# Second-part matmuls on 64 rows are widened to 128 rows in a float32r decoder layer

## The chip, the core and the metric

The kernel runs on one core of a Trainium2 chip. The metric is the device time of one execution in microseconds (us). The profile is of one execution on that core; a row of it names the engine (PE is TensorE's matmuls, PEld its weight loads, DVE is VectorE, ACT is ScalarE, POOL is GpSimd), the line of the kernel, the operation and the tiles out<-in.

## The reference, cut to what matters

One layer: RMSNorm, one wide input projection split into five branches, each branch with its own mixer, a gated merge, an output projection and a final RMSNorm. The tokens are 512, the model is 1024 wide, each branch 512. The change touches two of the branches.

```python
def stick_breaking_attention(q, k, v):          # 8 heads of 64 channels
    ...
        z = jnp.einsum('bhqd,bhkd->bhqk', qf[:, :, q0:tk], kf[:, :, :tk]) * scale
        ...
        later = lax.cumsum(log_keep, axis=3, reverse=True) - log_keep
        w = jnp.where(strict, jnp.exp(jax.nn.log_sigmoid(z) + later), 0.0)
        outs.append(jnp.einsum('bhqk,bhkd->bhqd', w, vf[:, :, :tk]))

def rg_lru(x, w_a, b_a, w_x, b_x, lam):         # 8 blocks of 64 channels
    xb = xf.reshape(b, s, NB_D, BW_D)
    r = jax.nn.sigmoid(jnp.einsum('bsnc,ncd->bsnd', xb, w_a.astype(jnp.float32)).reshape(b, s, e) + b_a)
    i = jax.nn.sigmoid(jnp.einsum('bsnc,ncd->bsnd', xb, w_x.astype(jnp.float32)).reshape(b, s, e) + b_x)
```

## The kernel before, in words

Every matmul operand is kept as two float32r parts, a first part (hi) and a second part (lo), whose sum is the float32 value. A product of two such values takes three matmuls in `mm3` (L178: hi by hi, L179: hi by lo, L180: lo by hi). Weights arrive by DMA as float32 (`wst`), ACT makes the first part (`whi`, L158) and DVE the second (`wlo`, L159); there are four buffers of each.

A string of steps (`STEPS`) lists the program's pieces in the order in which they are written: `bp0` to `bp3` project the queries, keys and gates of a pair of attention heads (`b_pair_proj`), `ba0` to `ba7` are the eight heads (`b_head`), `dt0` to `dt3` the four tiles of the RG-LRU gates (`d_tile`), `G` and `U` gate and up-projection steps of the merge, `cv`, `cp`, `ch` the mLSTM. A scheduler then interleaves the instructions of neighbouring steps on each engine by priority, so that the small matmuls of a head stand between the big ones of the merge. Each engine runs its list in order.

In `b_head` a head has 64 channels, which fill half of the 128 rows. The queries' tile `qq` holds the first part in the head's own half of the rows and the second part in the other half; the keys' tile `kk2` holds the first part in both halves. One matmul on 128 rows (L561) so gives the product of both parts of the queries with the first part of the keys. The product of the queries' first part and the keys' second part is a matmul on the head's own 64 rows (L562); the second parts of both heads of a pair share one tile, `kl`. A head has four such pairs of matmuls, of 512, 384, 128 and 256 columns, into `zb` banks. ACT makes sigmoids of the logits (L566 to L570), POOL masks them (L574), DVE runs the scan (L581) and the product (L582), PE transposes the weights of the attention (L591, into `wb`), ACT and DVE split them (L593, L594) into three hi and lo pairs of tiles, and PE multiplies them with the values (L605, into the single `po` bank).

The RG-LRU does the same with its blocks of 64 channels: `xx` holds both parts of a block's input in the two halves of the rows, `wh` the weights' first part in both halves, and L880 is a matmul on 128 rows, L881 the second part of the weights on 64. `d_setup` loads the weights into both halves of the rows and splits all 128 rows, so the second part already stands in both.

The tiles `q`, `k`, `kl` and the split attention weights come from one pool, `opool`, of 14 tiles of 128x512. Each evacuation in `b_pair_proj` works on 64 rows: L533 and L534 for the queries, L539, L540 (ACT) and L541 (DVE) for the keys.

Of the kernel before, what the change touches and what calls it, by code (L numbers as in the profile page):

```python
# [26 lines left out]
# section starts in w_in's columns  # L27
# [7 lines left out]
# channel-major column tiles of w_in, one [128, 8, 128] unit each  # L35
# [4 lines left out]
# columns of the packed per-channel constants  # L40
# [10 lines left out]
# blocks of the [key, query] triangle: key block j holds queries from 128 j on  # L51
TRI = {0: (0, 0, 512), 1: (1, 0, 384), 3: (1, 384, 128), 2: (2, 0, 256)}   # j: bank, offset, width
BANKW = (512, 512, 256)
PAIRS = [(i, j) for j in range(NT) for i in range(j, NT)]                  # (query block, key block)
# [27 lines left out]
def build(ctx, tc, x, memT, cols_d, rows_d, wcm, wbv, wcv0, wcv1, wmk, wmv, wup, wout, dw, fg, out):  # L82
# [14 lines left out]
    # ---------------------------------------------------------------- constants  # L97
# [14 lines left out]
    with tc.tile_pool(name="setup", bufs=1) as sp:  # L112
        t2 = sp.tile([P, P], F32, name="t_b")
        V.memset(t2, 1.0 / 512)
        V.tensor_copy(ones512, t2)
        t4 = sp.tile([P, P], F32, name="t_d")
        V.memset(t4, 0.0)
        # 0 where s <= t, -1e30 elsewhere   (partition s, free t)
        G.affine_select(out=cmask, in_=t4, pattern=[[1, P]], compare_op=ALU.is_ge, fill=-1e30, base=0,
                        channel_multiplier=-1)  # L120
# [9 lines left out]
    # ---------------------------------------------------------------- pieces  # L130
    def rsqrt(v, pool):
        """1 / sqrt(v) of a few columns, the table's root refined by a Newton step"""
        n = v.shape[1]
        s = pool.tile([P, n], F32, tag=f"rsq_s{n}", name="rsq_s", bufs=2)
        t = pool.tile([P, n], F32, tag=f"rsq_t{n}", name="rsq_t", bufs=2)
        act(s, v, AF.Sqrt, scale=0.25)
        V.reciprocal(t, s)
        V.tensor_tensor(out=t, in0=t, in1=v, op=ALU.mult)
        V.scalar_tensor_tensor(out=s, in0=t, scalar=0.25, in1=s, op0=ALU.mult, op1=ALU.add)
        V.reciprocal(t, s)  # L140
        return t
# [4 lines left out]
    def load_w(src, n, scale=None, stage=wpool):  # L146
        """a weight unit [128, n] in two halves of split operands: [(hi, lo), (hi, lo)]"""
# [19 lines left out]
    def piece(w, k, n, per, o=0, c=None):  # L167
        """columns of block k (n wide, per blocks in a half) of both parts"""
# [5 lines left out]
    def mm3(ps, terms, first=True, last=True, check=False):  # L174
        """terms: list of (lhsT hi, lhsT lo, rhs hi, rhs lo); three float32r passes each"""
# [6 lines left out]
    def proj(c, scale=None):  # L182
        """one 128-channel tile of the input projection, [channel, token], without its bias"""
# [10 lines left out]
    def split_sb(f, hi, lo):  # L194
        """f: float32 view of lo's own storage or another tile"""
# [13 lines left out]
    def vtile():  # L209
        """room for two split operands of 1024 columns (or mLSTM's values with their ones)"""  # L210
# [6 lines left out]
    # the array's clock rises after some microseconds of work: start it while the first loads run  # L217
# [4 lines left out]
    # ---------------------------------------------------------------- norms of mem and x  # L222
# [46 lines left out]
    # mem's projections take its rows' 1 / rms afterwards  # L269
# [73 lines left out]
    def op_pair():  # L343
        return op(), op()
# [19 lines left out]
    # ---------------------------------------------------------------- A: gated conv module  # L364
# [19 lines left out]
    def log_exp_tables(after):  # L384
        """one table set with both, loaded after the ACT instruction given"""
# [3 lines left out]
    def chan_mean(tiles, name):  # L389
        """mean over the channels of four tiles, on every partition"""  # L390
# [37 lines left out]
    # ---------------------------------------------------------------- M: memory attention  # L428
# [46 lines left out]
    # ---------------------------------------------------------------- token-major values  # L475
    def v_half(src, n):
        """[128 tokens, n] per token tile for n weight columns, without their bias"""
# [19 lines left out]
    # ---------------------------------------------------------------- B: stick-breaking attention  # L497
# [13 lines left out]
    def b_v(half):  # L511
        # per token tile and pair of heads: first parts of the even head, both second parts, first parts of the odd head
# [13 lines left out]
    def b_pair_proj(p):  # L526
        """per head 128 rows: the queries' two parts, and the keys' first part twice; and the keys' second parts"""
        q, k, kl = op_pair(), op_pair(), op()
# [8 lines left out]
        with tc.high_priority(offset=EVAC):  # L537
            for h, r in enumerate(HALF):
                act(k[h][r], ps[r], AF.Identity, bias=b[r])  # L539
                act(k[h][HALF[1 - h]], ps[r], AF.Identity, bias=b[r])  # L540
                V.scalar_tensor_tensor(out=kl[r], in0=ps[r], scalar=b[r], in1=f32(k[h][r]),  # L541
                                       op0=ALU.add, op1=ALU.subtract)
# [3 lines left out]
    def b_head(pp, hh):  # L546
        p, q, k, kl, z = pp
        qq, kk2 = q[hh], k[hh]
# [4 lines left out]
        for b, ts in enumerate(((3,), (2, 0), (1,))):  # L553
            # logits [query, key] of query blocks ts, keys up to the block's own
            z_ps = at.tile([P, S], F32, tag="at", name="zb")
            o = 0
            for t in ts:
# [4 lines left out]
                mm(d, lhsT=qq[r, tsl], rhs=kl[r, :n], start=False, stop=True, skip_group_check=True)  # L562
# [8 lines left out]
            for t in ts:                    # keys before the query alone  # L571
# [4 lines left out]
        for t in (3, 2, 0, 1):  # L576
# [3 lines left out]
            # products of what later keys leave, from the last key to the first (factors in [0, 1]: the min keeps them)  # L580
# [21 lines left out]
        for j in range(NT):                 # the head's rows take the values' first parts, the others the second  # L602
# [9 lines left out]
    # ---------------------------------------------------------------- C: mLSTM  # L612
# [4 lines left out]
    def c_v(half):  # L617
        # per token tile and head: values, ones (with a zero), the values' second part
# [23 lines left out]
    def c_gates():  # L642
        """running maxima, in-block sums of log f, and the exponents' two parts"""
# [14 lines left out]
        for t in range(NT):                # log f <= 0: the min keeps the sum  # L658
# [10 lines left out]
        # sums of whole blocks between key block j and query block i  # L669
# [157 lines left out]
    # ---------------------------------------------------------------- D: RG-LRU  # L827
    def d_rates(after):
        """8 log sigmoid(lambda), per channel"""
# [5 lines left out]
        # log1p(e) = 2 atanh(e / (2 + e)), e = exp(-|lam|) <= 1  # L835
# [16 lines left out]
    def d_setup():  # L852
        # per block of 64 channels both gates' weights side by side, first parts in both halves of the rows
# [9 lines left out]
    def d_tile(i):  # L863
# [9 lines left out]
        for b, h in enumerate(HALF):  # L873
            o = HALF[1 - b]
            xx = op()                       # both parts of a block's input
# [5 lines left out]
            mm(ps, lhsT=wl[h, sl], rhs=xx[h], start=False, stop=True)  # L881
# [8 lines left out]
    def d_scan(tiles):  # L890
        for i, r, ig, th, z in tiles:
            act(r, r, AF.Exp, scale=dst_["sc"][:, i:i + 1])
        # 1 - exp(2 l) = -tanh(l) (1 + exp(2 l))
# [16 lines left out]
    # ---------------------------------------------------------------- merge  # L910
# [29 lines left out]
    # ---------------------------------------------------------------- program  # L940
# [56 lines left out]
    # ---------------------------------------------------------------- output projection  # L997
# [31 lines left out]
    for half in range(2):  # L1029
        if half:  # L1030
            wo = [hl for k2 in range(4) for hl in load_out(1, k2)]
        for t in range(NT):
            tsl = slice(t * P, (t + 1) * P)
            parts = 2 if half and t == NT - 1 else 1          # the last tile in two
            w = S // parts
            for c in range(parts):
# [9 lines left out]
                # mean of squares so far, with eps  # L1046
# [17 lines left out]
def _layout(a):  # L1064
# [3 lines left out]
    def chan(v):                       # [n * 128] -> [128, n]  # L1068
        return v.reshape(-1, P).T
# [7 lines left out]
    def tok(s, n):                     # [2 halves of k, 128, 4, n]  # L1077
# [16 lines left out]
    def bd(w):                         # [8, 64, 64] -> [2, 64, 4, 64]: block 2 t + b at [b, :, t]  # L1094
# [26 lines left out]
```

## Time and profile before

| what | value |
|---|---|
| median of 3 runs | 866.03 us (865.93 to 866.09) |
| span of the profiled execution, first to last instruction | 864.6 us |
| PE busy | 853.6 us, 99% of the span |
| weight loads busy | 703.9 us, 81% |
| DVE busy | 624.3 us, 72% |
| ACT busy | 449.1 us, 52% |
| POOL busy | 38.7 us, 4% |
| mean granted TensorE clock | 0.997 |

The profiled execution's own time is its span, 864.6 us, and the little that lies around it; the median of the timed runs is 1.4 us above the span. Busy matmuls overlap in the profile, since a matmul's duration includes its way through the array, so the distance from one matmul's start to the next one's start says more than the duration.

### The profile page before, as it was taken

How to read it: one execution, taken by the hardware profiler on the slowest of the kernel's cores; microseconds unless marked ns; L12 is line 12 of the kernel's file. 1: busy time of each engine (PE TensorE's matmuls, PEld its weight loads, DVE VectorE, ACT ScalarE, POOL GpSimd, SP SyncE). 2: the span in 40 equal slices, each digit the busy share in tenths (PEclk: the TensorE clock that was granted, in tenths of full speed). 3: DMA queues.
4: the chain of work that ended last, by engine and by line, in shares of the span. 5: the costliest groups of instructions: out<-in, count | busy, mean ns of one | idle time of the engine just before them, and what ended most of it. 6: DMA issues, size and time to landing. Idle time of an engine off the chain costs nothing.

```text
span 864.6 us, 11346 instructions
## 1 busy us (share of the span) xinstructions
PE 853.6 (99%) x4100; PEld 703.9 (81%) x4100; DVE 624.3 (72%) x1198; ACT 449.1 (52%) x814; POOL 38.7 (4%) x83
## 2 busy tenths in 40 slices
PE   8999999999999999999999999999999999999996
PEld 7888888888898889777778888888888787788886
DVE  7979999999466587776676768668767665555744
ACT  5734456434364453566344445456355766763523
POOL 3000000000000111010231000000000000000000
PEclk9999999999999999999999999999999999999999
DMA  8332222222223121222122233332232222233612
GB/s 324 123 99 96 83 88 74 73 98 98 98 76 101 69 89 60 98 74 87 60 73 63 87 120 110 99 121 74 74 110 74 97 77 94 74 105 115 209 60 98
DMA packets 24145, 84.31 MB, mean 98 GB/s; under 512 B 2709, under 2 KB 2837, under 8 KB 24089
## 3 DMA queue, kind: packets, MB, share of 16 engines
q1 hardware_dynamic: 24088, 83.59, 28.4%
q8 instruction: 32, 0.52, 0.3%
q14 instruction: 25, 0.20, 0.1%
HBM read 81.47 MB, written 2.11 MB: 97 GB/s over the span
## 4 chain that ended last, share of the span: by engine, by line
PE 98%; DMA 1%; DVE 1%; ACT 0%; SPq 0%; issue 0%; ACTq 0%
PE pj L178 27%; PE pj L179 27%; PE pj L180 27%; PE pj L494 2%; PE pj L492 2%; PE pj L493 2%; PE zb L562 1%; PE po L605 1%; PE wb L591 1%; PE zb L561 1%; DMA mt<-in 1%; PE og L795 1%; PE pj L317 0%; PE pj L318 0%; PE tp L466 0%; PE dps L881 0%
## 5 line engine op out<-in xcount | busy, mean ns | idle before, releaser
L158 ACT ACTIVATE whi<-wst 128x512 fp32r<-128x512 f32 (+1 forms) x256 | 160.6, 631 | 287.5 <-PE pj L179 231.9
L179 PE MATMUL pj<-hL,whi 128*128 128x512 f32 x768 | 303.1, 395 | 0.0
L180 PE MATMUL pj<-hH,wlo 128*128 128x512 f32 x768 | 302.9, 395 | 0.0
L178 PE MATMUL pj<-hH,whi 128*128 128x512 f32 x768 | 302.8, 394 | 0.0
L159 DVE TENSOR_TENSOR wlo<-wst,whi 128x512 fp32r<-128x512 f32 (+1 forms) x256 | 176.6, 692 | 108.8 <-ACT whi L158 99.4
L180 PEld LDWEIGHTS pj<-hH,wlo 128*128 128x128 f32 x768 | 144.4, 188 | 33.5 <-issue 1.0
L179 PEld LDWEIGHTS pj<-hL,whi 128*128 128x128 f32 x768 | 144.4, 188 | 32.7 <-issue 0.5
L178 PEld LDWEIGHTS pj<-hH,whi 128*128 128x128 f32 x768 | 144.4, 188 | 32.4 <-issue 0.2
L380 DVE SCALAR_TENSOR_TENSOR acc<-u,cols,acc 128x512 f32<-128x512 f32 x120 | 88.1, 747 | 0.8
L178 PE MATMUL pj<-yH,whi 128*128 128x512 f32 x160 | 63.5, 398 | 0.0
L179 PE MATMUL pj<-yL,whi 128*128 128x512 f32 x160 | 63.0, 394 | 0.0
L180 PE MATMUL pj<-yH,wlo 128*128 128x512 f32 x160 | 62.9, 394 | 0.0
L178 PEld LDWEIGHTS pj<-yH,whi 128*128 128x128 f32 x160 | 30.0, 188 | 7.5 <-issue 0.5
L180 PEld LDWEIGHTS pj<-yH,wlo 128*128 128x128 f32 x160 | 30.1, 188 | 6.8
L179 PEld LDWEIGHTS pj<-yL,whi 128*128 128x128 f32 x160 | 30.1, 188 | 6.6
L574 POOL TENSOR_SCALAR_AFFINE_SELECT kp<-kp 128x128 f32<-128x128 f32 x32 | 14.3, 461 | 401.5 <-ACT kp L566 401.2
L581 DVE TENSOR_TENSOR_SCAN kp<-kp 128x512 f32<-128x512 f32 (+3 forms) x32 | 26.6, 854 | 7.5 <-POOL kp L574 7.3
L494 PE MATMUL pj<-whi,hL 128*128 128x256 f32 (+1 forms) x112 | 31.5, 283 | 0.0
L493 PE MATMUL pj<-wlo,hH 128*128 128x256 f32 (+1 forms) x112 | 31.5, 282 | 0.0
L492 PE MATMUL pj<-whi,hH 128*128 128x256 f32 (+1 forms) x112 | 31.3, 283 | 0.0
L922 ACT ACTIVATE g<-pj,cols 128x512 f32<-128x512 f32 x40 | 27.2, 679 | 2.1 <-DVE merged L938 1.5
L936 DVE TENSOR_TENSOR g<-g,pj 128x512 f32<-128x512 f32 x32 | 21.8, 682 | 8.6 <-PE pj L180 8.5
(306 smaller groups left out, 1188.0 us busy)
## 6 DMA issues: line engine op xcount, KB each, us to landing
wst<-in SPq DMA_DIRECT2D x138, 512.0 KB, 3.3
xt<-in SPq DMA_DIRECT2D x4, 512.0 KB, 10.6
merged<-in SPq DMA_DIRECT2D x4, 512.0 KB, 4.4
out<-merged SPq DMA_DIRECT2D x8, 256.0 KB, 2.3
wst<-in SPq DMA_DIRECT2D x2, 528.0 KB, 4.1
mt<-in SPq DMA_DIRECT2D x2, 512.0 KB, 5.8
f<-crow SPq DMA_DIRECT2D x4, 256.0 KB, 3.6
rows<-in SPq DMA_DIRECT2D x1, 518.0 KB, 10.3
```

Of the source, the lines that this page charges most:

```text
L158: act(hi[:, :m], f, AF.Copy)
L159: V.tensor_tensor(out=lo[:, :m], in0=f, in1=f32(hi[:, :m]), op=ALU.subtract)
L178: mm(ps, lhsT=ah, rhs=bh, start=first and i == 0, stop=False, skip_group_check=check)
L179: mm(ps, lhsT=ah, rhs=bl, start=False, stop=False, skip_group_check=check)
L180: mm(ps, lhsT=al, rhs=bh, start=False, stop=last and i == n - 1, skip_group_check=check)
L380: V.scalar_tensor_tensor(out=a, in0=u[:, k:k + S], scalar=col("a_w", i * 31 + k), in1=a, op0=ALU.mult, op1=ALU.add)
L492: mm(dst[t], lhsT=hH[:, k, tsl], rhs=wh, start=first, stop=False, skip_group_check=True)
L493: mm(dst[t], lhsT=hH[:, k, tsl], rhs=wl, start=False, stop=False, skip_group_check=True)
L494: mm(dst[t], lhsT=hL[:, k, tsl], rhs=wh, start=False, stop=k == NK - 1, skip_group_check=True)
L581: V.tensor_tensor_scan(kk, kk, kk, 1.0, op0=ALU.mult, op1=ALU.min)
L922: act(g, ps, AF.Sigmoid, bias=b)
L936: V.tensor_tensor(out=merged[:, d, :] if first else g, in0=g, in1=ps, op=ALU.mult)
```

## The change

The queries' tile and the RG-LRU's input tile are unchanged. The keys' second part gets a tile of its own for each head, in which it stands in both halves of the rows (two DVE instructions of 64 rows per head in place of one). L562 then takes all 128 rows of the queries (first and second part) and of the keys' second part, and L881 all 128 rows of the weights' second part and of the input. Each adds one product that was left out before, second part by second part. The rest of the diff takes comments out, which are not shown here.

```diff
     def b_pair_proj(p):
-        """per head 128 rows: the queries' two parts, and the keys' first part twice; and the keys' second parts"""
-        q, k, kl = op_pair(), op_pair(), op()
+
+        q, k, kl = op_pair(), op_pair(), op_pair()
...
             for h, r in enumerate(HALF):
                 act(k[h][r], ps[r], AF.Identity, bias=b[r])
                 act(k[h][HALF[1 - h]], ps[r], AF.Identity, bias=b[r])
-                V.scalar_tensor_tensor(out=kl[r], in0=ps[r], scalar=b[r], in1=f32(k[h][r]),
-                                       op0=ALU.add, op1=ALU.subtract)
+                for o in HALF:
+                    V.scalar_tensor_tensor(out=kl[h][o], in0=ps[r], scalar=b[r], in1=f32(k[h][r]),
+                                           op0=ALU.add, op1=ALU.subtract)
...
-        qq, kk2 = q[hh], k[hh]
+        qq, kk2, kl2 = q[hh], k[hh], kl[hh]
...
                 mm(d, lhsT=qq[:, tsl], rhs=kk2[:, :n], start=o == 0, stop=False, skip_group_check=True)
-                mm(d, lhsT=qq[r, tsl], rhs=kl[r, :n], start=False, stop=True, skip_group_check=True)
+                mm(d, lhsT=qq[:, tsl], rhs=kl2[:, :n], start=False, stop=True, skip_group_check=True)
...
             mm(ps, lhsT=wh[:, sl], rhs=xx, start=True, stop=False)
-            mm(ps, lhsT=wl[h, sl], rhs=xx[h], start=False, stop=True)
+            mm(ps, lhsT=wl[:, sl], rhs=xx, start=False, stop=True)
```

The changed kernel has one line more from L541 on, so the old L541 is L542 there, L561 and L562 are L562 and L563, L594 is L595, L605 is L606, and L881 is L882. The order of POOL's and SP's instructions is the same; on PE, ACT and DVE it differs around the attention branch. Three places follow.

On DVE, at the evacuation of the keys of the second pair of heads (`bp1`), the list before is:

```order
L534 SCALAR_TENSOR_TENSOR op<-pj,bq_99,op 64x512 x2
L159 TENSOR_TENSOR wlo<-wst,whi 128x512 x2
L541 SCALAR_TENSOR_TENSOR op<-pj,cols,op 64x512
L159 TENSOR_TENSOR wlo<-wst,whi 128x512
L541 SCALAR_TENSOR_TENSOR op<-pj,cols,op 64x512
L159 TENSOR_TENSOR wlo<-wst,whi 128x512
```

and with the change:

```order
L534 SCALAR_TENSOR_TENSOR op<-pj,bq_99,op 64x512 x2
L159 TENSOR_TENSOR wlo<-wst,whi 128x512 x2
L542 SCALAR_TENSOR_TENSOR op<-pj,cols,op 64x512 x2
L159 TENSOR_TENSOR wlo<-wst,whi 128x512
L542 SCALAR_TENSOR_TENSOR op<-pj,cols,op 64x512 x2
L159 TENSOR_TENSOR wlo<-wst,whi 128x512
```

Nothing moves there; each second part of the keys is made twice, in one go, between the same weight units.

On DVE again, in the first head that runs (`ba2`), these are the weight unit that PE's next big matmuls need (`wlo`, 528 columns), the last product of the scan, and the splits of the attention weights, with what each waits for. Before:

```order
L159 TENSOR_TENSOR wlo_2888<-wst_2885,whi_2887 128x528 [waits DMAHW4_49,Activation_49]
L582 TENSOR_TENSOR f_2745<-f_2745,kp02_589 128x256 [waits DVE_49,Pool_49]
L594 TENSOR_TENSOR op_2765<-wb_2759,op_2764 128x512 [waits Activation_49]
L594 TENSOR_TENSOR op_2774<-wb_2768,op_2773 128x512 [waits Activation_49]
L594 TENSOR_TENSOR op_2781<-wb_2777,op_2780 128x256 [waits Activation_49]
L159 TENSOR_TENSOR wlo_2892<-wst_2885,whi_2891 128x528 [waits Activation_49]
```

With the change:

```order
L159 TENSOR_TENSOR wlo_2894<-wst_2891,whi_2893 128x528 [waits DMAHW4_49,Activation_49]
L583 TENSOR_TENSOR f_2751<-f_2751,kp02_589 128x256 [waits DVE_49,Pool_49]
L595 TENSOR_TENSOR op_2771<-wb_2765,op_2770 128x512 [waits Activation_49]
L595 TENSOR_TENSOR op_2780<-wb_2774,op_2779 128x512 [waits Activation_49]
L595 TENSOR_TENSOR op_2787<-wb_2783,op_2786 128x256 [waits DVE_49,PE_49,Activation_49]
L159 TENSOR_TENSOR wlo_2898<-wst_2891,whi_2897 128x528 [waits Activation_49]
```

The third split now also waits for PE. Two pairs of heads hold two tiles more of the 14 than before, and the last tile of this head comes free only when the first value matmuls have read theirs.

On PE, a little later, this is the end of `ba2`'s value matmuls and the start of the next head's logits (`ba1`). Before:

```order
L605 MATMUL po<-op,v 128x384
L605 MATMUL po<-op,v 128x256
L494 MATMUL at<-whi,hL 128x264
L605 MATMUL po<-op,v 128x256
L605 MATMUL po<-op,v 128x128 x2
L492 MATMUL at<-whi,hH 128x264
L493 MATMUL at<-wlo,hH 128x264
```

With the change, the rows at the end of the same stretch are:

```order
L494 MATMUL at<-whi,hL 128x264
L562 MATMUL zb<-op 128x512
L606 MATMUL po<-op,v 128x256
L606 MATMUL po<-op,v 128x128 x2
L563 MATMUL zb<-op 128x512
L562 MATMUL zb<-op 128x384
```

The matmul of 256 columns that reads the late tile, and the two of 128 columns after it, move six big matmuls and one logit matmul down. In `ba6` they move down by eight big matmuls in the same way.

## Rows read from the trace of the kernel before

**Rows 1.** The page: span, busy time by engine, the chain that ended last.
```profile
span 864.6 us, 11346 instructions
...
PE 853.6 (99%) x4100; PEld 703.9 (81%) x4100; DVE 624.3 (72%) x1198; ACT 449.1 (52%) x814; POOL 38.7 (4%) x83
...
PE 98%; DMA 1%; DVE 1%; ACT 0%; SPq 0%; issue 0%; ACTq 0%
```

**Rows 2.** Timeline of PE, first head's logits: start us, duration us, line, tiles.
```profile
289.11 0.40 PE L561 MATMUL zb<-op 128*128 128x512 f32 x1
289.44 0.50 PE L562 MATMUL zb<-op 64*128 64x512 f32 x1
289.86 0.44 PE L561 MATMUL zb<-op 128*128 128x384 f32 x1
...
291.42 0.38 PE L562 MATMUL zb<-op 64*128 64x256 f32 x1
291.74 0.50 PE L178 MATMUL pj<-yH,whi 128*128 128x512 f32 x1
292.07 0.39 PE L179 MATMUL pj<-yL,whi 128*128 128x512 f32 x1
```

**Rows 3.** Timeline of the weight loads (PEld) at the same place.
```profile
288.88 0.19 PEld L561 LDWEIGHTS zb<-op 128*128 128x128 f32 x1
289.43 0.18 PEld L562 LDWEIGHTS zb<-op 64*128 64x128 f32 x1 [0.36 <-issue]
289.86 0.19 PEld L561 LDWEIGHTS zb<-op 128*128 128x128 f32 x1 [0.25 <-issue]
```

**Rows 4.** Timeline of PE, an mLSTM head's twelve score matmuls, three per width.
```profile
527.61 0.39 PE L769 MATMUL zb<-op 128*128 128x512 f32 x1
527.84 0.40 PE L770 MATMUL zb<-op 128*128 128x512 f32 x1
...
529.52 0.39 PE L178 MATMUL pj<-yH,whi 128*128 128x512 f32 x1
```

**Rows 5.** Timeline of PE, one RG-LRU block.
```profile
745.54 0.40 PE L880 MATMUL dps<-op,v 128*128 128x512 f32 x1
745.87 0.49 PE L881 MATMUL dps<-op,v 64*128 64x512 f32 x1
746.29 0.50 PE L180 MATMUL pj<-hH,wlo 128*128 128x512 f32 x1
746.63 0.39 PE L880 MATMUL dps<-op,v 128*128 128x512 f32 x1
```

**Rows 6.** Instructions of L562 and L881: count, ns least/median/most, first and last start, forms.
```profile
L562 PE MATMUL zb<-op x32: 323/409/498, 289.4 to 468.7; 64*128 64x512 f32 x8, 64*128 64x384 f32 x8, 64*128 64x128 f32 x8, 64*128 64x256 f32 x8
L881 PE MATMUL dps<-op,v x8: 491/492/502, 669.6 to 746.9; 64*128 64x512 f32 x8
```

**Rows 7.** Instructions of L541 and L534, the 64-row splits on DVE.
```profile
L541 DVE SCALAR_TENSOR_TENSOR op<-pj,cols,op x8: 741/750/758, 198.6 to 401.2; 64x512 fp32r<-64x512 f32 x8
L534 DVE SCALAR_TENSOR_TENSOR op<-pj,bq,op x8: 744/750/755, 192.9 to 392.2; 64x512 fp32r<-64x512 f32 x8
```

**Rows 8.** Timeline of DVE while the second pair's keys are evacuated.
```profile
280.11 0.74 DVE L541 SCALAR_TENSOR_TENSOR op<-pj,cols,op 64x512 fp32r<-64x512 f32 x1 [0.71 <-ACT op L540]
281.45 0.69 DVE L159 TENSOR_TENSOR wlo<-wst,whi 128x512 fp32r<-128x512 f32 x1 [0.60 <-ACT whi L158]
282.86 0.76 DVE L541 SCALAR_TENSOR_TENSOR op<-pj,cols,op 64x512 fp32r<-64x512 f32 x1 [0.71 <-ACT op L540]
```

**Rows 9.** Timeline of ACT, DVE and PE between the first head's logits and transposes.
```profile
289.69 0.67 ACT L922 ACTIVATE g<-pj,cols 128x512 f32<-128x512 f32 x1
290.26 0.59 ACT L566 ACTIVATE kp<-zb 128x512 f32<-128x512 f32 x1
...
296.69 0.70 DVE L159 TENSOR_TENSOR wlo<-wst,whi 128x528 fp32r<-128x528 f32 x1
...
297.84 0.37 PE L493 MATMUL pj<-wlo,hH 128*128 128x264 f32 x1
```

**Rows 10.** The same two ends in a later head: DVE's product, PE's transpose.
```profile
334.32 0.73 DVE L582 TENSOR_TENSOR f<-f,kp 128x384 f32<-128x384 f32 x2
...
337.16 0.27 PE L591 MATMUL wb<-ident,f 128*128 128x128 f32 x1
```

## The prediction

> **What bounds the kernel now.** I read the page first: PE is busy for 99% of the span, and the chain that ended last is PE for 98% of it [rows 1]. So a microsecond taken from PE's list counts as a microsecond of the end, as long as the others keep up. Busy time alone doesn't tell what PE loses, because matmuls overlap; so I went on to the timeline of PE around the lines that change and looked at the distance between starts. At full pace a 512-column matmul starts 0.23 us after the one before it: the mLSTM's L769 and L770 start at 527.61 and 527.84 [rows 4]. In the attention head the steps are longer. L562 (64 rows) starts 0.33 after L561, the next L561 (128 rows) 0.42 after that, and the first big matmul behind the group, L178, is followed only after 0.33 [rows 2]. The weight loads say why: the first L561, which follows another matmul on 128 rows, has its load begun at 288.88, 0.23 before it starts itself, so under the matmul before it; the load of L562 begins at 289.43, just as L562 starts, after 0.36 us in which the load side waited for nothing that the profile shows, and the load of the following L561 again waits 0.25 [rows 3]. So PE does not overlap across a change between 64 and 128 rows, in either direction. L562 runs 32 times and L881 8 times, all on 64 rows and all among matmuls on 128 [rows 6].
>
> **The change part by part.**
>
> *The switches.* First head: from the first L561 at 289.11 to L178 at 291.74 the eight logit matmuls take 2.63 us, and L178's own step is 0.10 longer than 0.23, together 2.73 [rows 2]. What the same eight take on 128 rows stands in the mLSTM: twelve matmuls of the same four widths, three of each, from 527.61 to 529.52, which is 1.91 [rows 4]. Two of three is 1.27. Saved: 2.73 - 1.27 = 1.46 us a head, 8 heads, 11.7. In some heads other small matmuls stand between the pairs; a pair then still has two switches, so I keep the figure. RG-LRU: L880, L881 and the matmul behind them take 0.33, 0.42 and 0.34, that is 1.09 [rows 5], against three steps of 0.23, 0.69 [rows 4]; saved 0.40 a block, 8 blocks, 3.2. Sum 14.9.
>
> The bounds. Above: if the narrow matmuls ran at the pace of the wide ones by columns (0.23 us for 512), the eight would take 1.15 and a head would save 1.58; with the RG-LRU 15.8. Below: if none of the 128- and 256-column matmuls could start closer than one weight load lasts, 0.19 [rows 3], and 384 neither, the eight would take 2 x (0.23 + 3 x 0.19) = 1.60 and a head would save 1.13, in all 12.2. I take 14.9, since the mLSTM rows are the same shapes on the same engine.
>
> A rule speaks against this gain. The row: a 64-row L881 costs its block 0.40 more than three equal steps [rows 5]. The Trainium skill, TensorE: Matmul & The Clock Gate, in its table on why this matters for your kernels, says that a single matmul over few rows takes the time of one over 128, and that the way to gain is to place several in distinct row groups so that they run at once. By that rule the width costs nothing either way and the sum would be 0; it is a rival below. The trace agrees with it for the matmul itself, not for its place between wider ones.
>
> *The second splits on DVE.* L541 was 8 x 0.75 us; now it is 16, the added eight into the other half of the rows. The trace has that form too: L534 reads one half and writes the other, also 0.75 [rows 7]. That is 6.0 us more of DVE in the whole run, against 0 on the path: in the second pair DVE sat idle for 0.71, 0.60 and 0.71 between these very instructions [rows 8], and each gap takes most of one. In the first pair DVE is full of convolution taps, which are behind by 3.0 us then; the order gives PE other steps there. If all of it came on the path it would cost 6.0; I take 0. ACT's work is unchanged, and `d_setup` did not change at all.
>
> *The extra tile.* A pair of heads now holds six of the 14 `opool` tiles. In `ba2` and `ba6` the third split of the attention weights waits for the head's own first value matmuls, and the order has moved its reader six or more matmuls down. That is over 1 us at 264 or 512 columns, and the split is one instruction on DVE. Queued behind it on DVE is the next weight half. I take 0, and price the other end as a rival.
>
> *Where PE now arrives early.* Between a head's logits and its transposes lies a way through ACT, POOL and DVE that gets no shorter. In `ba2` ACT is busy without a gap from 289.69 into the first sigmoid at 290.26, so this can't start earlier; DVE, in order behind the scans, makes the next `wlo` from 296.69 to 297.39, and PE uses it at 297.84, a lead of 0.45 [rows 9]. With PE 1.46 earlier, it waits 1.0. In `ba0`, the tightest of the other heads by what I read, DVE's product is done at 335.05 and its transpose starts at 337.16, a lead of 2.11 [rows 10], more than 1.46: nothing lost. So I give back 1.0 (at least 0, if the DVE row comes earlier too; at most 1.0 in each head, 8.0).
>
> Sum: 14.9 - 1.0 = 13.9. The profiled span goes from 864.6 [rows 1] to 850.7; the timed median is 1.4 above the span, so 852.1.
>
> **The rivals.**
>
> *The gain is given back in every head.* If the way through the other engines sets the pace of all eight heads as in `ba2`, 8.0 comes back: 14.9 - 8.0 = 6.9, that is 859.1. For it: the lead in `ba2` is only 0.45 [rows 9]. Against: the lead of 2.11 [rows 10], and DVE at 72%, ACT at 52% [rows 1].
>
> *The change does not do what it says.* If the long steps came from something that stays, such as two matmuls in a row into the same `zb` columns, or from the count of rows costing nothing as the rule has it, the time stays 866.0. Against: L769 and L770 add into the same columns too and keep 0.23 [rows 4], and the L178 behind L562, into another bank, is slow as well [rows 2].
>
> *Slower, by the late tile.* DVE works in order. If its third split in `ba2` and `ba6` held up the weight half behind it, and PE with it, the two places would have to cost (14.9 + 1.7) / 2 = 8.3 each to end 0.2% above now. That is all of the way from L562 at 289.44 [rows 2] to PE's use of the next weights at 297.84 [rows 9], 8.4; with 8.4 twice the time is 866.0 - 14.9 + 16.8 = 867.9. Against: what the split waits for is the first two value matmuls of the same head, which stand ahead of its reader on PE.
>
> **How the numbers follow.** A difference of 0.2%, 1.7 us, is about what a measurement of this kernel can tell from no change. My forecast, 850.0 to 855.5 around 852.1 (the two bounds of the switches less 1.0 or nothing give 850.2 and 854.8), has 0.83; the gain given back, 855.5 to 863, 0.09; no change 0.03; slower 0.02; better than 850.0, 0.03. The range 850.0 to 855.5 leaves out 0.17. Faster by over 0.2%: 0.83 + 0.09 + 0.03 = 0.95; same 0.03; slower 0.02.
>
> **What would show it.** Right: no matmul on 64 rows is left on PE; the eight logit matmuls of a head stand about 1.3 us apart from first to next big matmul, with no idle of the weight loads between them; L881's successor starts 0.23 after it; DVE is busy 6 us more; PE waits about 1 us in `ba2` for `wlo` and not in the later heads. Wrong: steps of 0.3 to 0.4 remain in the logits although all is on 128 rows (then the row count was not the cause), or PE shows waits on DVE before the transposes or the value matmuls of most heads (then the saving moved into the chain), or DVE's third split in `ba2` or `ba6` ends after PE wants it.

## The result, and the profile after

The changed kernel takes 852.42 us (median of 4 runs, 852.38 to 852.55); the kernel before, beside it on the same chip, 865.98 us (866.09 at most). The ratio is 0.9842, with a 95% interval of 0.9829 to 0.9854: 13.6 us less by the medians. The forecast was 852.1 us.

The page of the changed kernel: span, busy time by engine, and the chain that ended last, to be read against [rows 1].

```profile
span 850.6 us, 11359 instructions
...
PE 839.3 (99%) x4100; PEld 702.2 (83%) x4100; DVE 628.6 (74%) x1206; ACT 449.2 (53%) x814; POOL 40.5 (5%) x83
...
PE 96%; DVE 2%; DMA 1%; ACT 0%; issue 0%; POOL 0%; SPq 0%; DVEq 0%; POOLq 0%; ACTq 0%
```

The span is 14.0 us shorter and PE's busy time 14.3, with the same 4100 matmuls. PE is still busy for 99%, so it has nothing more to spare than before; its list has become shorter. The chain is 96% PE. In the first head it now leaves PE at 288.73, runs through ACT, POOL and DVE, and comes back with `wlo` at 296.80; that is where a part of the gain was given back (below).

The timeline of PE in the changed kernel, at the first head's logits (start us, duration us, line, tiles), answers to [rows 2].

```profile
288.79 0.39 PE L562 MATMUL zb<-op 128*128 128x512 f32 x1
289.02 0.39 PE L563 MATMUL zb<-op 128*128 128x512 f32 x1
...
290.07 0.40 PE L178 MATMUL pj<-yH,whi 128*128 128x512 f32 x1
290.30 0.39 PE L179 MATMUL pj<-yL,whi 128*128 128x512 f32 x1
```

The timeline of the weight loads at the same place answers to [rows 3].

```profile
288.79 0.19 PEld L563 LDWEIGHTS zb<-op 128*128 128x128 f32 x1
289.02 0.19 PEld L562 LDWEIGHTS zb<-op 128*128 128x128 f32 x1
```

The eight matmuls now take 288.79 to 290.07, 1.28 us. Before, they took 2.63, and 2.73 with the 0.10 by which the step of the L178 behind them was too long [rows 2]; that step is 0.23 now. Each weight load starts one step ahead of its matmul: that of L563 begins at 288.79, when L562 begins, and L563 itself at 289.02. The gaps of 0.36 and 0.25 in front of the loads are gone.

The timeline of PE in the changed kernel at the first and the last RG-LRU blocks; the last answers to [rows 5].

```profile
658.10 0.47 PE L881 MATMUL dps<-op,v 128*128 128x512 f32 x1
...
732.84 0.39 PE L881 MATMUL dps<-op,v 128*128 128x512 f32 x1
733.08 0.40 PE L882 MATMUL dps<-op,v 128*128 128x512 f32 x1
733.31 0.40 PE L178 MATMUL pj<-hH,whi 128*128 128x512 f32 x1
733.55 0.39 PE L179 MATMUL pj<-hL,whi 128*128 128x512 f32 x1
```

Three equal steps stand there now, 0.24, 0.23 and 0.24, where [rows 5] had 0.33, 0.42 and 0.34.

**Where the time came from.** The same instruction in both traces says how far ahead the changed kernel is. Two rows of PE's timeline are needed besides those shown, the first from the kernel before, the second from the changed kernel:

```profile
669.16 0.47 PE L880 MATMUL dps<-op,v 128*128 128x512 f32 x1
```

```profile
516.55 0.39 PE L770 MATMUL zb<-op 128*128 128x512 f32 x1
```

The first logit matmul starts at 289.11 [rows 2] and at 288.79: 0.32 ahead, before any changed matmul. That is scatter between executions: two more traces of the changed kernel (experiments 6 and 12) have it at 289.35 and 288.83. The first mLSTM score matmul starts at 527.61 [rows 4] and at 516.55: 11.06. So the attention stage gave 10.74. The first RG-LRU matmul started at 669.16 before and starts at 658.10: still 11.06, nothing lost or won between. The eighth block's starts at 746.63 [rows 5] and 732.84: 13.79, so seven blocks gave 2.73, 0.39 each; eight give 3.1. PE's last matmul is 13.93 ahead, since 0.23 is lost again soon after the last block. In the changed kernel a weight load of L178 waits 0.44 there for ACT's L923, which stands behind a table load, and its matmul starts at 744.90, 0.40 after the one before it in place of 0.23. The other two traces of the changed kernel have the same step; in the kernel before PE came there later and did not wait.

**Where some of it went.** Timeline of PE in the changed kernel where the first head's transposes come (the bracket is the idle time before, and what ended it); it answers to the last row of [rows 9].

```profile
296.24 0.33 PE L592 MATMUL wb<-ident,f 128*128 128x128 f32 x1
296.85 0.39 PE L493 MATMUL pj<-wlo,hH 128*128 128x264 f32 x1 [0.29 <-DVE wlo L159]
```

The timeline of DVE just before.

```profile
294.27 0.66 DVE L937 TENSOR_TENSOR merged<-g,pj 128x512 f32<-128x512 f32 x1
294.85 0.68 DVE L582 TENSOR_TENSOR_SCAN kp<-kp 128x256 f32<-128x256 f32 x1
295.45 0.73 DVE L583 TENSOR_TENSOR f<-f,kp 128x384 f32<-128x384 f32 x2
296.10 0.70 DVE L159 TENSOR_TENSOR wlo<-wst,whi 128x528 fp32r<-128x528 f32 x1
```

PE wants `wlo` and DVE ends it at 296.80; L493 follows at 296.85. The bracket counts only 0.29 as idle, because it begins at the end that the profile gives the matmul before (296.24 + 0.33); by starts PE loses more. The L179 behind the logits was at 292.07 [rows 2] and is at 290.30: 1.77 ahead. L493 was at 297.84 [rows 9] and is at 296.85: 0.99 ahead. Between them 0.78 is given back. About 0.2 of it lies ahead of L592, the head's first transpose, which starts at 296.24 when DVE has ended two of the head's products at 296.18; the rest lies ahead of L493.

### The profile page after: what moved, and what is told of

It is laid out like the page before. It is cut to its first block, busy times and chain, and to the rows that moved or that the text cites. A ratio compares the mean times of both kernels' runs of the same rounds, so it can differ in the third digit from the quotient of the medians.

```text
span 850.6 us, 11359 instructions
## 1 busy us (share of the span) xinstructions
PE 839.3 (99%) x4100; PEld 702.2 (83%) x4100; DVE 628.6 (74%) x1206; ACT 449.2 (53%) x814; POOL 40.5 (5%) x83
## 3 DMA queue, kind: packets, MB, share of 16 engines
HBM read 81.47 MB, written 2.11 MB: 98 GB/s over the span
## 4 chain that ended last, share of the span: by engine, by line
PE 96%; DVE 2%; DMA 1%; ACT 0%; issue 0%; POOL 0%; SPq 0%; DVEq 0%; POOLq 0%; ACTq 0%
PE pj L180 27%; PE pj L178 27%; PE pj L179 27%; PE pj L493 1%; PE pj L494 1%; PE pj L492 1%; PE po L606 1%; PE wb L592 1%; PE og L796 1%; PE zb L563 1%; DMA mt<-in 1%; PE zb L562 1%; PE pj L317 0%; DVE memL L265 0%; PE pj L318 0%; PE tp L466 0%
## 5 line engine op out<-in xcount | busy, mean ns | idle before, releaser
L180 PE MATMUL pj<-hH,wlo 128*128 128x512 f32 x768 | 303.0, 395 | 0.0
L178 PE MATMUL pj<-hH,whi 128*128 128x512 f32 x768 | 303.0, 395 | 0.0
L179 PE MATMUL pj<-hL,whi 128*128 128x512 f32 x768 | 302.7, 394 | 0.0
L180 PEld LDWEIGHTS pj<-hH,wlo 128*128 128x128 f32 x768 | 144.5, 188 | 32.6
L179 PEld LDWEIGHTS pj<-hL,whi 128*128 128x128 f32 x768 | 144.6, 188 | 32.0
L178 PEld LDWEIGHTS pj<-hH,whi 128*128 128x128 f32 x768 | 144.6, 188 | 31.7
L179 PE MATMUL pj<-yL,whi 128*128 128x512 f32 x160 | 63.2, 395 | 0.0
L178 PE MATMUL pj<-yH,whi 128*128 128x512 f32 x160 | 63.1, 395 | 0.0
L180 PE MATMUL pj<-yH,wlo 128*128 128x512 f32 x160 | 63.0, 395 | 0.0
L178 PEld LDWEIGHTS pj<-yH,whi 128*128 128x128 f32 x160 | 30.1, 188 | 6.9 <-ACT g L923 0.4
L179 PEld LDWEIGHTS pj<-yL,whi 128*128 128x128 f32 x160 | 30.1, 188 | 6.7
L180 PEld LDWEIGHTS pj<-yH,wlo 128*128 128x128 f32 x160 | 30.1, 188 | 6.7
L575 POOL TENSOR_SCALAR_AFFINE_SELECT kp<-kp 128x128 f32<-128x128 f32 x32 | 16.4, 524 | 392.4 <-ACT kp L567 392.1
L493 PE MATMUL pj<-wlo,hH 128*128 128x256 f32 (+1 forms) x112 | 31.5, 282 | 0.3 <-DVE wlo L159 0.3
L494 PE MATMUL pj<-whi,hL 128*128 128x256 f32 (+1 forms) x112 | 31.4, 282 | 0.0
L492 PE MATMUL pj<-whi,hH 128*128 128x256 f32 (+1 forms) x112 | 31.3, 283 | 0.0
L923 ACT ACTIVATE g<-pj,cols 128x512 f32<-128x512 f32 x40 | 27.1, 678 | 3.3 <-PE pj L180 1.6
L937 DVE TENSOR_TENSOR g<-g,pj 128x512 f32<-128x512 f32 x32 | 21.8, 681 | 8.2 <-PE pj L180 8.1
```

Source lines behind the costliest of these rows:

```text
L178: mm(ps, lhsT=ah, rhs=bh, start=first and i == 0, stop=False, skip_group_check=check)
L179: mm(ps, lhsT=ah, rhs=bl, start=False, stop=False, skip_group_check=check)
L180: mm(ps, lhsT=al, rhs=bh, start=False, stop=last and i == n - 1, skip_group_check=check)
L492: mm(dst[t], lhsT=hH[:, k, tsl], rhs=wh, start=first, stop=False, skip_group_check=True)
L493: mm(dst[t], lhsT=hH[:, k, tsl], rhs=wl, start=False, stop=False, skip_group_check=True)
L494: mm(dst[t], lhsT=hL[:, k, tsl], rhs=wh, start=False, stop=k == NK - 1, skip_group_check=True)
```

## The experiments

Theory: PE pays for each change between 64- and 128-row matmuls, because the weight load then waits for the matmul before it; 64 changes in attention and 16 in the RG-LRU. First rival: it pays for something else that the changed lines have (64 rows as such, two matmuls in a row into the same `zb` columns), or the gain comes from the rearranged DVE and tiles. Second rival: the saving is given back in every head. Ratios are to the kernel before, run beside it on the same chip, with 95% intervals.

**1. The attention alone** (the changed kernel with the RG-LRU's line as before).

```diff
-            mm(ps, lhsT=wl[:, sl], rhs=xx, start=False, stop=True)
+            mm(ps, lhsT=wl[h, sl], rhs=xx[h], start=False, stop=True)
```

> The changed kernel, but with the RG-LRU's second-part matmul back on 64 rows; only the attention's logits are widened. Switch theory (each change between 64 and 128 rows costs PE about 0.18 us, and the attention had 64 of them): 866.0 - 11.7 + 1.0 = 855.3, range 854.8 to 855.9. Rival, the parts don't add (a wait that the RG-LRU's speed-up only shifted): over 0.7 away from that, and the other part alone does not make up the rest.

Measured: 855.37 us, ratio 0.9875 (0.9859 to 0.9892); the kernel before took 866.39 beside it. 11.0 us.

**2. The RG-LRU alone** (the kernel before with that line changed the other way).

> The kernel before, with only the RG-LRU's second-part matmul on 128 rows; no instruction is added on any engine. Switch theory: 16 switches less, 2.9 (as the trace of the changed kernel has it) to 3.2 saved, 862.8 to 863.1. Rival, a 64-row matmul costs no more than one on 128 rows and the gain of the change lies in the attention's data: 866.0.

Measured: 863.46 us, ratio 0.9964 (0.9951 to 0.9977), 2.9 us. The two parts add up: 11.0 + 2.9 = 13.9, where the whole change gave 13.4 to 13.8 in its three measurements (the result, experiments 6 and 12).

**3. Fewer changes, the same matmuls.** The kernel before, all second-part matmuls on 64 rows, but those of a head collected behind its four 128-row ones.

```diff
-                mm(d, lhsT=qq[r, tsl], rhs=kl[r, :n], start=False, stop=True, skip_group_check=True)
+                seconds.append((d, tsl, n))
...
+        for d, tsl, n in seconds:
+            mm(d, lhsT=qq[r, tsl], rhs=kl[r, :n], start=False, stop=True, skip_group_check=True)
```

> The kernel before, with the logit matmuls of a head written in two groups: the four on 128 rows first, then the four on 64. All 32 stay on 64 rows with the same operands; the order on PE has 14 stretches of 64-row matmuls in place of 32, so 28 switches in place of 64. Switch theory: 36 x 0.18 = 6.6 saved, 859.4, less some tenths that come back as waits, because the first sigmoids start later; range 858.8 to 861. Rival, the 64 rows themselves are slow (each such matmul costs its 0.19 twice wherever it stands): 866.0, range 865.5 to 867.

Measured: 860.70 us, ratio 0.9935 (0.992 to 0.9949), 5.7 us. The timeline of PE in this kernel, first head:

```profile
289.80 0.80 PE L562 MATMUL zb<-op 128*128 128x512 f32 x4
290.52 0.90 PE L568 MATMUL zb<-op 64*128 64x512 f32 x4
291.36 0.50 PE L178 MATMUL pj<-yH,whi 128*128 128x512 f32 x1
291.69 0.39 PE L179 MATMUL pj<-yL,whi 128*128 128x512 f32 x1
```

The same eight matmuls take 289.80 to 291.36, and 0.10 more in L178's step: 1.66 us, against 2.73 in pairs [rows 2] and 1.28 on 128 rows. Two changes cost 0.38 here, where eight cost 1.45. So the 64 rows as such do not cost it: inside the two stretches the matmuls of 384 and of 128 columns take steps of 0.175 and 0.060 us on 64 rows as on 128. This run also takes apart the two matmuls into the same `zb` columns; that these are not the cause is seen in the changed kernel, where L563 still follows L562 into the same columns and the step is 0.23. The changes of row count are left, 0.18 to 0.19 us each. The scheduler cut the eight heads' collections into 14 stretches, 28 changes in place of 64. 36 x 0.18 = 6.5, and a wait of about half a microsecond in `ba2` as in the changed kernel leaves 6.0, near the 5.7.

**4. The second splits alone.** The changed kernel's splits and tiles, both matmuls on 64 rows.

```diff
-                mm(d, lhsT=qq[:, tsl], rhs=kl2[:, :n], start=False, stop=True, skip_group_check=True)
+                mm(d, lhsT=qq[r, tsl], rhs=kl2[r, :n], start=False, stop=True, skip_group_check=True)
```

> The changed kernel's DVE work and its extra tile per pair (the keys' second part in both halves of the rows), but both second-part matmuls on 64 rows as before. Theory (the 6.0 us of DVE and the later tile are hidden): 866.0, range 865.6 to 866.8. Rival, the added splits or the tile cost time on the path, covered in the changed kernel by the gain: up to 6.0 more, 867 to 872.

Measured: 866.06 us, ratio 0.9998 (0.9988 to 1.0007). DVE's busy time is 630.3 us, 6.0 more than in [rows 1], and the time does not move (the interval is about 0.1% either way): the splits and the extra tiles are free beside PE's old list, and none of the gain comes from them.

**5. The RG-LRU's second part as two 64-row matmuls**, one on each half of the rows, the other half's into a bank that nothing reads.

```diff
-            mm(ps, lhsT=wl[:, sl], rhs=xx, start=False, stop=True)
+            mm(ps, lhsT=wl[h, sl], rhs=xx[h], start=False, stop=True)
+            other = at.tile([P, S], F32, tag="at", name="dpo")
+            mm(other, lhsT=wl[o, sl], rhs=xx[o], start=True, stop=True)
```

> The changed kernel, with the RG-LRU's second-part matmul cut into two of 64 rows, one on each half of the rows, the second into a bank of its own that nothing reads (so the product of that half is left out of the result). A block then has two switches again, 8 x 0.36 = 2.9, and one matmul more. If matmuls in different row groups run at once, as the Trainium skill has it (TensorE: Matmul & The Clock Gate, packing small matmuls), the two start together: 855.3. If they run one behind the other at full pace: 8 x 0.23 more, 857.1. If the change of half is a switch like that of the row count: 8 x 0.18 more again, 858.6.

Measured: 855.42 us, ratio 0.987 (0.9854 to 0.9887), within 0.1 us of experiment 1 with its single 64-row matmul. The timeline of PE in this kernel, first two blocks:

```profile
658.71 0.47 PE L881 MATMUL dps<-op,v 128*128 128x512 f32 x1
659.11 0.49 PE L882 MATMUL dps<-op,v 64*128 64x512 f32 x1
659.12 0.49 PE L884 MATMUL dpo<-op,v 64*128 64x512 f32 x1
659.54 0.50 PE L881 MATMUL dps<-op,v 128*128 128x512 f32 x1
```

The two halves start within 0.01 us of each other and the next matmul follows 0.43 after the first, as behind one alone [rows 5]. They run at once, and together they pay for two changes, as one alone does.

**6. The changed kernel again**, for the next two to stand against.

> The changed kernel once more, as the mark for the three that follow on the same chip: 852.4, range 852.0 to 852.8.

Measured: 852.86 us (852.77 to 852.91), ratio 0.9844 (0.9831 to 0.9856).

**7. A filler step moved into the first head**, to cover its wait (in the list of steps).

```diff
-G4 U4 az3 an0 G4 G0 ao0 bv0 az2 az1 bp1 G0 ao2 ao3 ao1 ba2 U4 cv1 ba1 G0 U0 U4 ba0 U0 bv1 U0
+G4 U4 az3 an0 G4 G0 ao0 bv0 az2 az1 bp1 G0 ao2 ao3 ao1 ba2 U4 G0 cv1 ba1 U0 U4 ba0 U0 bv1 U0
```

> The changed kernel with one gate step of the merge moved from behind the second head to between the first head and the mLSTM's values, so that PE has 24 big matmuls more between the first head's logits and its transposes. Theory (the 0.76 us that PE loses in the first head is PE arriving before the way through ACT, POOL and DVE is done): that wait goes, 851.7, range 851.4 to 852.0. Rival, the wait moves to the next step that DVE is late for: 852.4, and the trace shows it at another line.

Measured: 859.88 us (857.57 to 860.97), ratio 0.9921 (0.9908 to 0.9934): 7.0 us above the changed kernel, a miss. The wait in `ba2` went, but the next head was left without the big matmuls that had covered it. The timeline of PE in this kernel, in that head, and the first transpose of a later one (`ba3`):

```profile
320.70 0.30 PE L592 MATMUL wb<-ident,f 128*128 128x128 f32 x1 [1.58 <-DVE f L583]
321.81 0.39 PE L492 MATMUL pj<-whi,hH 128*128 128x256 f32 x1 [0.81 <-DVE merged L937]
...
324.62 0.63 PE L180 MATMUL pj<-yH,wlo 128*128 128x512 f32 x1
325.05 0.63 PE L178 MATMUL pj<-yH,whi 128*128 128x512 f32 x1
...
387.53 0.45 PE L592 MATMUL wb<-ident,f 128*128 128x128 f32 x1 [2.33 <-DVE lq L847]
```

Busy time in windows of this kernel (start and end, length in us, then PE, PEld, DVE, ACT and POOL busy with their instructions, PE's granted clock as a share of 2.4 GHz, DMA share, GB/s):

```profile
318.00:322.00 4.00, 1.61 (x7) 0.89 (x6) 4.00 (x9) 0.86 (x3) 1.95 (x4) 1.00 0.00 0
322.60:326.00 3.40, 3.40 (x14) 3.01 (x13) 1.28 (x3) 0.00 (x0) 0.00 (x0) 0.51 0.39 151
```

And two windows over nearly the same stretch of the changed kernel:

```profile
318.00:322.00 4.00, 4.00 (x24) 3.39 (x23) 4.00 (x8) 2.59 (x5) 0.29 (x1) 1.00 0.28 87
322.00:326.00 4.00, 4.00 (x23) 3.44 (x21) 3.95 (x6) 1.26 (x2) 0.00 (x0) 1.00 0.26 102
```

In the changed kernel PE is busy for all of 318 to 322; here for 1.61 of 4.00, while DVE is busy throughout, with the head's scans and products and other steps' work between them. PE's first transpose waits 1.58 for a product, and L492 then 0.81 for the merge product. After these waits the granted clock is 0.51, the lower level of 1.2 GHz, and matmuls of 512 columns start 0.43 apart instead of 0.23. So a wait is paid twice: as idle time and as a slow stretch behind it.

The moved step does not explain the whole loss by its own head. A third wait, 2.33, stands in `ba3`, and behind it the granted clock is 0.53 from 387.60 to 391.00. The scheduler had rearranged the lists there too: ACT loads function tables 43 times in this kernel, 41 times in the changed one. The six executions show the two payments apart. Two took 857.57 and 857.83 at a mean granted clock of 0.996, which is that of the changed kernel beside them; one took 859.10 at 0.994; three took 860.66 to 860.97 at 0.992. So some 4.8 us of the loss are there at the changed kernel's clock, and some 3 more come with the lower one (an estimate, since only one of the six, at 860.97, has a trace).

**8. The ten 4-row transposes in one stretch.** L693 and L695 are transposes on 4 rows among 128-row matmuls, and the only matmuls on fewer than 128 rows that are left. A copy on DVE that the first of them needs holds them back until all can run.

```diff
+        V.tensor_copy(tps[:4, :1], a2(9)[:, :1])
```

> The changed kernel with the mLSTM's ten transposes on 4 rows (L693) held back by one small DVE copy until all their inputs are there, so that they and the four of L695 stand in one stretch on PE in place of three. Switch theory, carried to a change between 128 and 4 rows: two stretches less, 4 x 0.18 = 0.7 saved, 851.7, range 851.4 to 852.1. Rival, the price belongs to 64 rows, or the transposes now come late for the mLSTM: 852.4 or more.

Measured: 851.99 us (851.88 to 852.26), ratio 0.9834 (0.9821 to 0.9847), 0.9 below experiment 6, and inside the expected range. The timeline of PE in the changed kernel, where they stand in three stretches:

```profile
357.85 0.39 PE L179 MATMUL pj<-hL,whi 128*128 128x512 f32 x1
358.17 0.29 PE L693 MATMUL tps<-ident,f 4*128 4x4 f32 x2
358.39 0.50 PE L180 MATMUL pj<-hH,wlo 128*128 128x512 f32 x1
358.72 0.40 PE L178 MATMUL pj<-hH,whi 128*128 128x512 f32 x1
...
359.74 0.22 PE L693 MATMUL tps<-ident,f 4*128 4x4 f32 x1
...
361.95 0.59 PE L693 MATMUL tps<-ident,f 4*128 4x4 f32 x7
```

And in this kernel, in one:

```profile
362.53 0.78 PE L694 MATMUL tps<-ident,f 4*128 4x4 f32 x10
363.18 0.38 PE L696 MATMUL tps<-ident,f 4*128 4x4 f32 x4
363.49 0.51 PE L179 MATMUL pj<-hL,whi 128*128 128x512 f32 x1
```

Entering and leaving show the signs of [rows 2]: 0.32 from L179 to the transposes and 0.33 from L180 to L178, against 0.23. Two stretches less are four changes; 4 x 0.18 = 0.7 was expected. The traces show 0.5: from the first logit matmul to the first mLSTM score the changed kernel takes 227.74 to 227.76 us in its three traces and this one 227.24, so 0.13 for each change. The rest of the 0.9 is of the size of the scatter.

**9. Both of these edits.**

> Both of the last two edits together. Theory: they lie in different stages and add, 851.0, range 850.6 to 851.5. Rival: no sum, as one of them gains nothing, 851.7 or more.

Measured: 862.93 us, ratio 0.9959 (0.9946 to 0.9972), a miss, by waits before the transposes as in experiment 7, here the longest 5.8 us, in `ba3`. Two rows of ACT's timeline ahead of that wait:

```profile
383.29 1.28 ACT L840 ACT_TABLE_LOAD   x1
...
384.81 1.28 ACT L567 ACT_TABLE_LOAD   x1
```

The two loads stand between the head's first sigmoids and the others (1.28 us each), and this kernel has 46 table loads against 41. So the cover that was moved is not the only thing that changed; how much of the loss is the table loads, no run separates.

**10. The weights of `cv1` ahead of the merge step.** Another way at the wait in `ba2`: the late `wlo` stood behind `merged` (L937) and the scans on DVE.

```diff
-G4 U4 az3 an0 G4 G0 ao0 bv0 az2 az1 bp1 G0 ao2 ao3 ao1 ba2 U4 cv1 ba1 G0 U0 U4 ba0 U0 bv1 U0
+G4 U4 az3 an0 G4 G0 ao0 bv0 az2 az1 bp1 G0 ao2 ao3 ao1 ba2 cv1 U4 ba1 G0 U0 U4 ba0 U0 bv1 U0
```

> The changed kernel with the step cv1 (values of the mLSTM's second half) written ahead of U4 behind the first head ba2. On DVE both halves of that weight unit are then split before the head's scans, and the merge product that stood between the scans moves behind the head; on PE the up-projection's matmuls move from before the transposes of ba2 into the next head. If the 0.76 us that PE's steps lose in ba2 come from the late second part of that weight unit on DVE, they go, and the time is 0.7 us under the changed kernel in the same call, about 851.7 to 852.2. Rival: the wait only moves to the next head, where the up-projection now stands between the logits: same time as the changed kernel, or some us more with waits before the transposes, as in the earlier move of a filler step (859.9).

Measured: 852.72 us (852.64 to 853.33), ratio 0.9845 (0.9832 to 0.9858): as the changed kernel beside it (experiment 12). The timeline of PE in this kernel, then that of DVE:

```profile
296.04 0.28 PE L494 MATMUL pj<-whi,hL 128*128 128x264 f32 x1
296.55 1.45 PE L592 MATMUL wb<-ident,f 128*128 128x128 f32 x10 [0.23 <-DVE f L583]
297.75 0.37 PE L492 MATMUL at<-whi,hH 128*128 128x264 f32 x1
```

```profile
293.23 1.40 DVE L582 TENSOR_TENSOR_SCAN kp<-kp 128x384 f32<-128x384 f32 x2
295.00 0.75 DVE L582 TENSOR_TENSOR_SCAN kp<-kp 128x256 f32<-128x256 f32 x1 [0.37 <-POOL kp L575]
295.68 1.06 DVE L583 TENSOR_TENSOR f<-f,kp 128x384 f32<-128x384 f32 x3
```

No matmul waits for `wlo` there any more; the transposes wait instead, for the head's own products. L592 comes 0.51 after L494, whose step is 0.12 elsewhere, and the ten transposes take 1.20 to the next start, in later heads, where they stand together, 1.01: 0.58 lost. On DVE the merge product is gone from between the scans, and DVE now waits 0.37 there for POOL's masks. So what sets this head's end is the way through ACT, POOL and DVE, as the chain of the changed kernel says too; the late `wlo` was one place where it showed.

**11. That move, with the 4-row transposes in one stretch.**

> The same move, with the ten 4-row transposes in one stretch. If both savings add: 0.7 + 0.9 = 1.6 us under the changed kernel, about 851. Rival: the move costs as in the earlier one, and the time is above the changed kernel's.

Measured: 852.21 us (852.07 to 852.43), ratio 0.9838 (0.9824 to 0.9851): 0.5 below experiment 10.

**12. The changed kernel a third time.**

> The changed kernel once more, for the two others to stand against on the same chip: 852.4 to 852.9.

Measured: 852.52 us (852.32 to 852.85), ratio 0.9842 (0.9829 to 0.9856).

The lowest median is that of experiment 8. In both pairs (8 against 6, 11 against 10) every run with the transposes together lies below every run without, and the medians are 0.9 and 0.5 us apart; against experiment 12 it is 0.3, and the runs overlap. All this is under the 0.2% that these measurements tell from no change, and the ratios' intervals overlap: a faster version than the changed kernel is not shown.

## Why the prediction was right, step by step

*PE sets the end.* Right. The span fell by 14.0 and PE's busy time by 14.3, at the same 99%.

*The switches.* Right in mechanism and size. 1.28 us for a head's eight matmuls against a forecast of 1.27; 1.45 saved in the first head (1.77 less the 0.32 from before) against 1.46; and 0.39 a block in the RG-LRU against 0.40. Over all heads it is (10.74 + 0.78) / 8 = 1.44 each. Experiments 1 and 2 split the gain into 11.0 and 2.9, where the forecast had 11.7 - 1.0 = 10.7 and 3.2. Experiment 3 shows that it is the change of row count that costs: the same 64-row matmuls, collected, save 5.7 without being widened. The Trainium skill, TensorEngine Tiling (Array Packing), section Key Properties, says that changing the tiling mode drains TensorE. The trace agrees as far as it shows this: across a change the weight load begins within 0.01 us of its own matmul, not a step ahead [rows 3]; that the array is empty by then, no row shows. The price is 0.18 to 0.19 us a change here.

*The rule that spoke against it.* It holds for the matmuls and not for the list. Experiment 5's two 64-row matmuls on different halves run at once, as the Trainium skill, TensorE: Matmul & The Clock Gate, Part 3: Packing small matmuls, has it. That a 64-row matmul takes the time of one on 128 rows is seen in experiment 3, inside the stretches; the prediction's own rows do not show it (L562's 0.50 against L561's 0.40 [rows 2]). What does not follow is that the width costs nothing here: that rival fell with experiments 1 to 3. Packing as such was not run. The two blocks of a tile have their second parts in different halves, so the pair could stand together, but it would still pay for two changes, some 0.37 us by experiment 3's figure (an estimate), where 128 rows pay for none.

*The second splits and the extra tile.* Right: 6.0 us more on DVE, 0 in the time (experiment 4). In the changed kernel the busy time is only 4.3 us higher; the added eight splits take 0.75 each there too, but more of DVE's rows overlap. The rival that the late tile would make it slower has no support: DVE does stand for 1.21 us before the third split in `ba2`, but PE waits for L595 neither there nor in `ba6`.

*Where PE arrives early.* Right in place and kind, a little too dear: `ba2` gives back 0.78 where 1.0 was forecast. The forecast held DVE's end of `wlo` fixed at 297.39; it came at 296.80, 0.59 earlier, with 0.32 of that the head start from before the first logits. The other 0.27 was PE's own doing. In the kernel before, the merge product, which stands ahead of the last scan and `wlo` on DVE, had waited for a PE matmul that now comes earlier:

```profile
294.83 0.69 DVE L936 TENSOR_TENSOR merged<-g,pj 128x512 f32<-128x512 f32 x1 [0.16 <-PE pj L180]
```

The later heads lose nothing, as said: no matmul there starts late for want of another engine. The lead shrinks and stays. In `ba0`, where it was 2.11 [rows 10], DVE's product now ends at 332.22 and the first transpose starts at 333.19, a lead of 0.97:

```profile
331.49 0.73 DVE L583 TENSOR_TENSOR f<-f,kp 128x384 f32<-128x384 f32 x2
```

```profile
333.19 0.27 PE L592 MATMUL wb<-ident,f 128*128 128x128 f32 x1
```

The big matmuls between a head's logits and transposes are that lead; where some were moved away from `ba1`, the first transpose waited 1.58 (experiment 7). Experiment 10 names what is behind the `ba2` wait: take the weight unit away from DVE's queue and the transposes wait in its place, so most of the 0.78 is the head's own way through the engines and not that one split.

What the sum missed: the 0.23 that PE loses to ACT after the last RG-LRU block, the same kind of early arrival at a place that the prediction did not look at, and 0.32 of scatter that fell on the favourable side of the profiled execution. That the two losses, 0.78 and 0.23, add up to the 1.0 that was forecast for `ba2` alone is luck. A hit within 0.3 us is more than the sum could promise: the changed kernel's own medians are 852.42, 852.86 and 852.52.

Left open: how experiment 9's loss divides between idle time, table loads and the lower clock, and why the wait in `ba3` came up in experiment 7.

## What to carry to other kernels

A lone matmul on 64 rows among full ones costs two changes, some 0.36 to 0.39 us here, for 128 to 512 columns alike; look for it as steps of 0.33 to 0.42 where 0.23 is usual in the timeline of PE, beside weight loads that wait for nothing the profile shows, and either fill the missing rows with data that does no harm, or collect the narrow ones in one stretch. When PE's list gets shorter, count for each head what lies between its first matmul and the one that needs the other engines' answer, because that cover shrinks with it (2.11 to 0.97 in `ba0`). Do not move cover from one place to another without counting it at both, and look at what else the scheduler moved: here the place that lost it also paid in clock.

## What the runs showed of the hardware that was not expected

- 4-row transposes show the same longer steps at entry and exit (0.32 and 0.33 us) as 64-row matmuls; put together they saved 0.13 us a change, against 0.18 to 0.19 for 64 rows.
- Two 64-row matmuls in different halves start within 0.01 us and together take what one takes (experiment 5).
- After PE had been busy for 1.61 of 4.00 us, its granted clock was 0.51 from 322.60 to 326.00 with PE fully busy (experiment 7); in the changed kernel it stayed at 1.00 there.
- Idle time in brackets understates what PE loses: 0.29 shown in `ba2`, 0.78 by the distance between starts.
